# A fused encoder block on one core: order and engines of the first pair's weight splits in a Strassen-like FFN

## The chip, the cores and the metric

The kernel runs on one core of a Trainium2 chip. The metric is the device time of one execution in microseconds (us). The engines are PE (TensorE, with PEld for its weight loads), DVE (VectorE), ACT (ScalarE), POOL (GpSimd) and SP (SyncE, which here issues every DMA). Each engine works through its own list of instructions in order.

## The reference, cut to what matters

One layer: a norm, a projection into an attention part and a convolution part, their joint output projection, then the gated FFN that this change touches, and a gated embedding after it.

```python
x = x + mix @ w_out[i]
h = rmsnorm(x, ffn_norm[i])
x = x + (jax.nn.silu(h @ w_gate[i]) * (h @ w_up[i])) @ w_down[i]
gate = jax.nn.sigmoid(rmsnorm(x, ple_norm[i]) @ w_ple_gate[i])
x = x + gate * (p[i] @ w_ple_proj[i])
```

`x` is 1024 positions by 1024, all in float32; the hidden width of the FFN is 2816.

## The kernel before

**Precision.** A float32 product is made of three matmuls. `split` (L68 to L74) takes a float32 operand apart: the high part is a cast on ACT (L71), the low part a subtraction (L74) on DVE, or on POOL where the call says so. `mm3` (L78 to L80) multiplies high by high, high by low and low by high into one PSUM bank. L78 and L79 read only the high part of a weight; L80 reads its low part.

**The output projection, L673 to L709.** Eight tiles of 128 positions, t = 0 to 7. Each gets its product with `w_out` (PE), the sum with the stored half (DVE, L684), the norm (ACT L647, DVE L106, POOL L107, DVE L649). Tiles 4 to 7 are combined with tiles 0 to 3 on POOL (L702 to L705, four instructions for each), and `tsplit` transposes the results on PE (L655) and splits them into the operands B11, B21, T1, T2, T3, T4 and B22.

**The FFN's gate and up products, L731 to L823.** The hidden width is walked in 11 pairs of 128-wide blocks, p = 0 to 10. Each pair does the two products (w = 0 gate, w = 1 up) as a 2 by 2 block product with seven instead of eight block multiplications. Its weight blocks are a11, a12, a21, a22 (L737 loads them, each as two DMAs of 256 KB), its sums s1 to s4 (DVE, L752, L753, L759, L761). The products are X = a11·B11, Y = s2·T2, X += a12·B21, Z = s1·T1, Y += s3·T3, Z += s4·B22, Y += a22·T4, each for both w, 12 matmuls each. After a11·B11 the bank X is copied to `e1` by ACT (L778), before a12·B21 adds to it. Then come sums of the banks on DVE (L781, L792, L793, L796, L799), the activations, and stores. At the end of each pair, two rows of `w_down` (tiles `wd`) are loaded (L816), combined by four DVE instructions (L818 to L821) and stored (L823).

**Buffers.** Raw weight tiles have the tag `raw`, four buffers, shared by the x1 tiles of the output projection (before p = 0), the four blocks and the two `wd` tiles. Split weight tiles have the tag `whl`, eight buffers, shared by the split `w_out` blocks and by the h and l parts of a11 to s4; so four operands are held at a time. The combination tiles s1 to s4 use the tag `y`, four buffers, which hold the normed tiles 0 to 3 until these are transposed. `tm` (with `e1`) is opened after `sp3` is closed and lies over its memory; each of its tiles waits for what lies under it.

**Order.** The order of each engine's list is fixed when the kernel is built. A planner walks a simulated timeline: on each engine, of the instructions that are ready there, the one written earliest in the program goes first. So the program order is a priority, and an instruction that is ready early in the plan fills a gap. On the chip the list is run in that order, ready or not.

In the first pair (p = 0) alone, all low parts are made by POOL:

```python
            split(h, l, src, None, nc.gpsimd if p == 0 else None)
```

Of the kernel before, what the change touches and what calls it, by code (L numbers as in the profile page):

```python
# [8 lines left out]
F32 = mybir.dt.float32  # L9
F32R = mybir.dt.float32r  # L10
# [7 lines left out]
P = 128  # L18
# [33 lines left out]
def hybrid_block(ctx: ExitStack, tc: tile.TileContext, I, out):  # L52
    nc = tc.nc
    dma = nc.sync.dma_start
# [4 lines left out]
    def f32(ap):  # L59
        return ap.bitcast(F32)  # L60
# [4 lines left out]
    def sb_pool(name, side=None):  # L65
        return tc.tile_pool(name=name, bufs=1, side=side, reuse_waits="tile")

    def split(h, l, src, eng_h=None, eng_l=None):  # L68

        if eng_h is None:  # L70
            nc.scalar.copy(h, src)  # L71
        else:
            eng_h.tensor_copy(h, src)
        (eng_l or nc.vector).tensor_sub(l, src, f32(h))  # L74
# [447 lines left out]
    for h in range(NH):  # L522
# [11 lines left out]
        for c in range(2):  # L534
# [14 lines left out]
            for pr_ in range(2):  # L549
# [40 lines left out]
                if fi >= 0:  # L590
                    n = 16 - fi if h * 4 + c * 2 + pr_ == 15 else 1
# [32 lines left out]
    def tbank(name):  # L624
        bankn[0] = (bankn[0] + 1) % 4
        return bank(name, (P, 4, P), 4 + bankn[0])
# [12 lines left out]
    raws = es4.enter_context(sb_pool("raws", side="right"))  # L639
# [3 lines left out]
    sp3 = es3.enter_context(sb_pool("sp3"))  # L643
# [7 lines left out]
    def tsplit(src, hl, tt, name):  # L651

        tp = tbank(name)
        for k in range(4):
            nc.tensor.transpose(tp[:, k, :], src[:, k * P:(k + 1) * P], ident)  # L655
        ts_ = slice(tt * P, (tt + 1) * P)
        split(hl[0][:, :, ts_], hl[1][:, :, ts_], tp)
# [8 lines left out]
    def op_pair(pool, name, tag, bufs):  # L666
        return [pool.tile([P, 4, 512], F32R, name=name + w, tag=tag, bufs=bufs) for w in "hl"]


    B = {n: op_pair(mcp, n, "act", 4) for n in ("B11", "B21")}  # L670
    B |= {n: op_pair(bx, n, "bx", 6) for n in ("T2", "T1", "B22")}
    xns = []
    for t in range(NT):  # L673
        half, tt = t // 4, t % 4
        a = slice(tt * P, (tt + 1) * P)
        x1 = raws.tile([P, D], F32, name=f"x1_{t}", tag="raw", bufs=4)
        dma(x1, part_d[t * P:(t + 1) * P, :])
        for ch in range(2):
            cs = slice(ch * 512, (ch + 1) * 512)
            ps = mbank(f"po{ch}{t}")  # L680
            for k in range(NH):
                wh, wl = wsets[ch][1](k)
                mm3(ps, mA[0][half][:, k, a], mA[1][half][:, k, a], wh, wl, k == 0, k == NH - 1)
            nc.vector.tensor_add(x1[:, cs], ps, x1[:, cs])  # L684
        dma(x1_d[t], x1)
        if half == 0:
            xn = cvy.tile([P, D], F32, name=f"n2_{t}_xn", tag="y", bufs=4)
            xns.append(xn)
        else:
            xn = sp3.tile([P, D], F32, name=f"n2_{t}_xn", tag="xin", bufs=2)  # L690
        xnorm(x1, gain2, xn, sp3, f"n2_{t}")
        lo, hi = xn[:, 0:512], xn[:, 512:D]
        if half == 0:
            tsplit(lo, B["B11"], tt, f"b11_{t}")
            tsplit(hi, B["B21"], tt, f"b21_{t}")
            continue
        if tt == 0:
            B["T3"] = op_pair(map_, "T3", "act", 4)
        xa = xns[tt]
        alo, ahi = xa[:, 0:512], xa[:, 512:D]  # L700
        t2 = sp3.tile([P, 512], F32, name=f"t2_{t}", tag="t2", bufs=2)
        nc.gpsimd.tensor_sub(alo, lo, alo)  # L702
        nc.gpsimd.tensor_sub(t2, hi, alo)
        nc.gpsimd.tensor_sub(lo, hi, lo)
        nc.gpsimd.tensor_sub(ahi, ahi, t2)  # L705
        tsplit(t2, B["T2"], tt, f"tt2_{t}")
        tsplit(alo, B["T1"], tt, f"tt1_{t}")
        tsplit(lo, B["T3"], tt, f"tt3_{t}")
        tsplit(hi, B["B22"], tt, f"b22_{t}")  # L709
    B["T4"] = op_pair(map_, "T4", "act", 4)  # L710
    for tt in range(4):
        tsplit(xns[tt][:, 512:D], B["T4"], tt, f"tt4_{tt}")
# [8 lines left out]

    es5 = ExitStack()
    tm = es5.enter_context(sb_pool("tm"))
    wgs = [I[n][0].rearrange("(k p) c -> p k c", p=P) for n in ("w_gate", "w_up")]
    wds = I["w_down"][0]
    V = nc.vector

# [2 lines left out]

    for p in range(NPR):  # L731

        def blk(i, k):
            r = raws.tile([P, 2, 4, P], F32, name=f"wr{p}{i}{k}", tag="raw", bufs=4)
            f = 2 * p + i
            for w in range(2):
                dma(r[:, w], wgs[w][:, 4 * k:4 * k + 4, f * P:(f + 1) * P])  # L737
            return r

        def sop(src, name):  # L740
            h = whl.tile([P, 2, 4, P], F32R, name=f"{name}h{p}", tag="whl", bufs=8)
            l = whl.tile([P, 2, 4, P], F32R, name=f"{name}l{p}", tag="whl", bufs=8)
            split(h, l, src, None, nc.gpsimd if p == 0 else None)
            return h, l

        def comb(name):
            return cvy.tile([P, 2, 4, P], F32, name=f"{name}_{p}", tag="y", bufs=4)

        a11, a22, a21 = blk(0, 0), blk(1, 1), blk(1, 0)
        A = {"a11": sop(a11, "a11")}  # L750
        s1, s2 = comb("s1"), comb("s2")
        V.tensor_add(s1, a21, a22)  # L752
        V.tensor_sub(s2, s1, a11)  # L753
        A["s2"] = sop(s2, "s2")
        a12 = blk(0, 1)
        A["a12"] = sop(a12, "a12")
        A["s1"] = sop(s1, "s1")
        s3, s4 = comb("s3"), comb("s4")
        V.tensor_sub(s3, a11, a21)  # L759
        A["s3"] = sop(s3, "s3")  # L760
        V.tensor_sub(s4, a12, s2)  # L761
        A["s4"] = sop(s4, "s4")
        A["a22"] = sop(a22, "a22")

        def prod(ps, a, b, w, first):
            for k in range(4):
                mm3(ps, A[a][0][:, w, k, :], A[a][1][:, w, k, :], B[b][0][:, k, :], B[b][1][:, k, :],
                    first and k == 0, k == 3, not first)

        gu = range(2)  # L770
        X = [bank(f"X{p}{w}") for w in gu]
        Y = [bank(f"Y{p}{w}") for w in gu]
        e1 = [tmp(f"e1{p}{w}", f"e1{w}", 2) for w in gu]
        aa = [tmp(f"aa{p}{w}", f"aa{w}") for w in gu]
        bb = [tmp(f"bb{p}{w}", f"bb{w}") for w in gu]
        for w in gu:
            prod(X[w], "a11", "B11", w, True)
            nc.scalar.copy(e1[w], X[w])  # L778
        for w in gu:
            prod(Y[w], "s2", "T2", w, True)  # L780
            V.tensor_add(aa[w], Y[w], e1[w])  # L781
        for w in gu:
            prod(X[w], "a12", "B21", w, False)
        g11 = tmp(f"g11{p}", "g11")
        nc.scalar.activation(g11, X[0], AF.Silu)
        V.tensor_mul(g11, X[1], g11)
        Z = [bank(f"Z{p}{w}") for w in gu]
        for w in gu:
            prod(Z[w], "s1", "T1", w, True)
        for w in gu:  # L790
            prod(Y[w], "s3", "T3", w, False)
            V.tensor_add(bb[w], Y[w], e1[w])  # L792
            V.tensor_add(bb[w], Z[w], bb[w])  # L793
        for w in gu:
            prod(Z[w], "s4", "B22", w, False)
            V.tensor_add(aa[w], Z[w], aa[w])  # L796
        for w in gu:
            prod(Y[w], "a22", "T4", w, False)
            V.tensor_add(e1[w], Y[w], e1[w])  # L799

        for c in (bb, aa, e1):
            nc.scalar.activation(c[0], c[0], AF.Silu)
            V.tensor_mul(c[1], c[0], c[1])
        g22, g12, g21 = bb[1], aa[1], e1[1]

        h1, h2, h3, h4 = [tmp(f"h{i}_{p}", "hs", 4) for i in range(4)]
        V.tensor_add(h1, g12, g22)
        V.tensor_sub(h2, h1, g11)
        V.tensor_sub(h3, g11, g12)
        V.tensor_sub(h4, g21, h2)  # L810
        for i, g in enumerate((g11, g21, g22, h1, h2, h3, h4)):
            dma(ga_d[i][p], g)
        d0 = raws.tile([P, D], F32, name=f"wd{p}0", tag="raw", bufs=4)
        d1 = raws.tile([P, D], F32, name=f"wd{p}1", tag="raw", bufs=4)
        for i, d in enumerate((d0, d1)):
            dma(d, wds[(2 * p + i) * P:(2 * p + i + 1) * P, :])  # L816
        b11, b12, b21, b22 = d0[:, 0:512], d0[:, 512:D], d1[:, 0:512], d1[:, 512:D]
        V.tensor_sub(b11, b12, b11)  # L818
        V.tensor_sub(b12, b22, b12)
        V.tensor_sub(b22, b22, b11)  # L820
        V.tensor_sub(b21, b21, b22)  # L821
        for i, b in enumerate((b11, b22, b12, b21)):
            dma(wb_d[i][p], b)  # L823
# [6 lines left out]
    sp3 = es3.enter_context(sb_pool("sp3b", side="right"))  # L830
# [100 lines left out]
    A = {n: pair(n) for n in ("pa11", "pa12")}  # L931
    A["pa22"] = pair("pa22", ap)
    f11, f12, f21, fs1 = block("f11"), block("f12"), block("f21"), block("fs1")
    for t in range(NT):
# [3 lines left out]
        for k in range(2):  # L938
# [3 lines left out]
            if t < 4:  # L942
                h, l = A[("pa11", "pa12")[k]]
# [4 lines left out]
            else:  # L948
                V.tensor_add(fs1[:, :, ts_], tp, f21[:, :, ts_])
                h, l = A["pa22"]  # L950
# [139 lines left out]
```

## Time and profile before

| What | us |
|---|---|
| median of 3 runs (1289.46 to 1292.21) | 1291.48 |
| the profiled execution, its own time | 1289.18 |
| its span, first to last instruction | 1287.4 |
| PE busy | 1249.3 |
| DVE busy | 937.5 |
| POOL busy | 394.4 |

The span is the device time without 1.8 us at its ends. Times in the views are counted from the start of the span. A busy PE is not a PE at its best: matmuls overlap, and the clock that the chip grants it can be half.

### The profile page before, as it was taken

The numbers are of one execution on the slowest core, as the hardware profiler recorded it, in microseconds if no ns is written. First come the engines' busy times: TensorE is split into PE (matmuls) and PEld (weight loads), VectorE is DVE, ScalarE is ACT, GpSimd is POOL, SyncE is SP. The second block draws the span as 40 slices with busy tenths as digits, with TensorE's granted clock in tenths as the row PEclk, the third lists the DMA queues.
The fourth block names the chain that finished last, engine by engine and source line by source line (L and its number), as shares of the span: only waits on it lengthen the run. The fifth ranks groups of instructions, "written<-read, shape, count | busy, mean of one in ns | idle before, by whom it ended". The sixth has DMA issues, their size and how long they took to land.

```text
span 1287.4 us, 16537 instructions
## 1 busy us (share of the span) xinstructions
PE 1249.3 (97%) x5945; PEld 1021.1 (79%) x5945; DVE 937.5 (73%) x1220; ACT 583.0 (45%) x862; POOL 394.4 (31%) x237
## 2 busy tenths in 40 slices
PE   8999998989999999987999999999999999999998
PEld 6788877867887888866888888888888788888886
DVE  7548999868887885877667676667665576567797
ACT  7445565445776673442223232223232444346552
POOL 2459998576667661660000000000000000000230
PEclk9999999989999999988999999999999999999999
DMA  9731232496655243445444445444454997665445
GB/s 356 240 88 50 66 107 74 127 225 176 154 126 149 76 134 121 172 131 180 146 165 147 156 164 172 147 161 147 152 171 166 385 349 234 191 196 176 135 147 164
DMA packets 165079, 213.12 MB, mean 166 GB/s; under 512 B 12088, under 2 KB 90182, under 8 KB 164997
## 3 DMA queue, kind: packets, MB, share of 16 engines
q1 hardware_dynamic: 164996, 212.06, 52.0%
q8 instruction: 47, 0.77, 0.3%
q14 instruction: 36, 0.29, 0.1%
HBM read 146.41 MB, written 65.60 MB: 165 GB/s over the span
## 4 chain that ended last, share of the span: by engine, by line
PE 81%; DVE 7%; DMA 6%; issue 2%; POOL 2%; ACT 1%; SPq 1%; DVEq 0%; POOLq 0%; ACTq 0%
PE Y L78 5%; PE Y L79 5%; PE Y L80 5%; PE Z L79 3%; PE Z L78 3%; PE Z L80 3%; PE X L80 3%; PE X L78 3%; PE X L79 3%; PE dY L78 2%; PE dY L79 2%; PE dY L80 2%; PE s L562 2%; DVE acc L351 2%; PE s L563 2%
## 5 line engine op out<-in xcount | busy, mean ns | idle before, releaser
L107 POOL TENSOR_TENSOR n_r<-n_ss,mhalf 128x1 f32<-128x1 f32 x24 | 14.7, 617 | 670.1 <-DVE n_ss L106 661.6
L74 DVE TENSOR_TENSOR dl<-dr,dh 128x1024 fp32r<-128x1024 f32 x77 | 93.7, 1224 | 62.6 <-ACT dh L71 62.4
L71 ACT CAST dh<-dr 128x1024 fp32r<-128x1024 f32 x77 | 80.5, 1049 | 105.9 <-PE dY L80 37.2
L356 POOL TENSOR_TENSOR z<-z,pr 128x1024 f32<-128x1024 f32 x45 | 115.8, 2575 | 3.2 <-ACT pr L355 0.8
L351 DVE SCALAR_TENSOR_TENSOR acc<-u,cw,acc 128x1024 f32<-128x1024 f32 x71 | 91.2, 1285 | 1.5
L570 ACT ACTIVATE e<-s,nm 128x1024 f32<-128x1024 f32 x64 | 71.6, 1119 | 35.9 <-DVE nm L567 29.6
L567 DVE TENSOR_REDUCE nm<-s 128x1 f32<-128x1024 f32 x64 | 77.3, 1219 | 9.1 <-PE s L565 4.5
L579 POOL TENSOR_TENSOR e<-e,e 128x1024 f32<-128x1024 f32 x32 | 77.8, 2431 | 2.4
L355 ACT ACTIVATE pr<-u,cw 128x1024 f32<-128x1024 f32 x45 | 51.1, 1150 | 36.0 <-POOL z L356 35.6
L562 PE MATMUL s<-ka,qa 128*128 128x512 f32 x128 | 57.3, 448 | 1.6 <-ACT e L570 1.5
L578 POOL TENSOR_SCALAR e<-e,cf 128x1024 f32<-128x1024 f32 x32 | 36.9, 1153 | 65.0 <-DVE cf L577 31.9
L79 PE MATMUL dY<-dl,dh 128*128 128x512 f32 x132 | 51.5, 390 | 0.0
L563 PE MATMUL s<-kb,qb 80*128 80x512 f32 x128 | 51.4, 402 | 0.0
L80 PE MATMUL dY<-dh,dl 128*128 128x512 f32 x132 | 51.4, 389 | 0.0
L78 PE MATMUL dY<-dh 128*128 128x512 f32 x132 | 50.3, 391 | 0.0
L74 DVE TENSOR_TENSOR wtl<-wt,wth 128x512 fp32r<-128x512 f32 x64 | 43.2, 683 | 8.9 <-ACT wth L71 8.6
L71 ACT CAST wth<-wt 128x512 fp32r<-128x512 f32 x64 | 36.8, 587 | 20.6 <-PE wt L584 20.5
L796 DVE TENSOR_TENSOR aa<-Z,aa 128x512 f32<-128x512 f32 x22 | 15.2, 690 | 38.5 <-PE Z L80 38.3
L80 PE MATMUL X<-B11h,a11l 128*128 128x512 f32 x88 | 33.5, 401 | 6.5 <-DVE a11l L74 6.5
L79 PE MATMUL av<-wtl,avh 128*128 128x256 f32 x128 | 38.4, 300 | 0.0
L584 PE MATMUL wt<-ident,e 128*128 128x128 f32 x256 | 37.5, 273 | 0.3 <-DVE wtl L74 0.2
L78 PE MATMUL av<-wth,avh 128*128 128x256 f32 x128 | 37.5, 293 | 0.2 <-ACT wth L71 0.2
(396 smaller groups left out, 3984.9 us busy)
## 6 DMA issues: line engine op xcount, KB each, us to landing
dr<-ga_d SPq DMA_DIRECT2D x77, 256.0 KB, 5.6
wr<-in_w_gate SPq DMA_DIRECT2D x44, 256.0 KB, 3.0
wr<-in_w_up SPq DMA_DIRECT2D x44, 256.0 KB, 3.5
wd<-in_w_down SPq DMA_DIRECT2D x22, 512.0 KB, 3.5
wb_d<-wd SPq DMA_DIRECT2D x44, 256.0 KB, 2.0
ga_d<-h SPq DMA_DIRECT2D x44, 256.0 KB, 3.6
dr<-wb_d SPq DMA_DIRECT2D x44, 256.0 KB, 3.4
dr<-in_w_down SPq DMA_DIRECT2D x33, 256.0 KB, 3.1
```

The source lines that it names most:

```text
L71: nc.scalar.copy(h, src)
L74: (eng_l or nc.vector).tensor_sub(l, src, f32(h))
L78: nc.tensor.matmul(ps, lh, rh, start=first, stop=False, skip_group_check=more)
L79: nc.tensor.matmul(ps, lh, rl, start=False, stop=False, skip_group_check=more)
L80: nc.tensor.matmul(ps, ll, rh, start=False, stop=last, skip_group_check=more)
L351: nc.vector.scalar_tensor_tensor(acc, u[:, k:k + S], cw[:, j, k:k + 1], acc, ALU.mult, ALU.add)
L356: nc.gpsimd.tensor_add(y2, y2, pr)
L562: nc.tensor.matmul(o, qa[:, m, ts_], ka[:, m, kc * 512:(kc + 1) * 512], start=True, stop=False)
L563: nc.tensor.matmul(o, qb[:, m, ts_], kb[:, m, kc * 512:(kc + 1) * 512], start=False, stop=not diag)
L567: nc.vector.tensor_reduce(nm, sp, AX.X, ALU.max, negate=True)
L570: nc.scalar.activation(e, sp, AF.Exp, bias=nm, accum_out=s)
L579: nc.gpsimd.tensor_add(es[0], es[0], es[1])
```

## The change

In the first pair only. (1) The block a11 is loaded and split in the program right after tile t = 7's transposes, ahead of those of T4, into two tiles of its own (tag `a11`, in `sp3`) instead of two of `whl`; its low part stays on POOL. (2) The block a12 is loaded and split right after it, ahead of a22, a21 and the sums. (3) Of the low parts only that of s2 (and that of a11) stays on POOL; those of a12, s1, s3, s4 and a22 go to DVE. (4) On PE, the products a12·B21 follow directly on a11·B11, ahead of s2·T2. The other ten pairs keep their text.

```diff
+    wgs = [I[n][0].rearrange("(k p) c -> p k c", p=P) for n in ("w_gate", "w_up")]
+
+    def blk(p, i, k):
+
+        r = raws.tile([P, 2, 4, P], F32, name=f"wr{p}{i}{k}", tag="raw", bufs=4)
+        f = 2 * p + i
+        for w in range(2):
+            dma(r[:, w], wgs[w][:, 4 * k:4 * k + 4, f * P:(f + 1) * P])
+        return r
+
     xns = []
     for t in range(NT):
...
         tsplit(hi, B["B22"], tt, f"b22_{t}")
+    a11s = [sp3.tile([P, 2, 4, P], F32R, name=f"a11{w}0", tag="a11", bufs=2) for w in "hl"]
+    a11_0 = blk(0, 0, 0)
+    split(*a11s, a11_0, None, nc.gpsimd)
     B["T4"] = op_pair(map_, "T4", "act", 4)
...
         def sop(src, name):
             h = whl.tile([P, 2, 4, P], F32R, name=f"{name}h{p}", tag="whl", bufs=8)
             l = whl.tile([P, 2, 4, P], F32R, name=f"{name}l{p}", tag="whl", bufs=8)
-            split(h, l, src, None, nc.gpsimd if p == 0 else None)
+            split(h, l, src, None, nc.gpsimd if p == 0 and name == "s2" else None)
             return h, l
...
-        a11, a22, a21 = blk(0, 0), blk(1, 1), blk(1, 0)
-        A = {"a11": sop(a11, "a11")}
+        a11 = blk(p, 0, 0) if p else a11_0
+        A = {"a11": sop(a11, "a11") if p else a11s}
+        if p == 0:
+            a12 = blk(p, 0, 1)
+            A["a12"] = sop(a12, "a12")
+        a22, a21 = blk(p, 1, 1), blk(p, 1, 0)
         s1, s2 = comb("s1"), comb("s2")
         V.tensor_add(s1, a21, a22)
         V.tensor_sub(s2, s1, a11)
         A["s2"] = sop(s2, "s2")
-        a12 = blk(0, 1)
-        A["a12"] = sop(a12, "a12")
+        if p:
+            a12 = blk(p, 0, 1)
+            A["a12"] = sop(a12, "a12")
         A["s1"] = sop(s1, "s1")
...
         for w in gu:
             prod(X[w], "a11", "B11", w, True)
             nc.scalar.copy(e1[w], X[w])
+
+        for w in gu:
+            if p == 0:
+                prod(X[w], "a12", "B21", w, False)
         for w in gu:
             prod(Y[w], "s2", "T2", w, True)
             V.tensor_add(aa[w], Y[w], e1[w])
         for w in gu:
-            prod(X[w], "a12", "B21", w, False)
+            if p:
+                prod(X[w], "a12", "B21", w, False)
```

## Rows read from the trace of the kernel before

**Rows 1.** The page's shares: busy us, share of the span, instructions.
```profile
PE 1249.3 (97%) x5945; PEld 1021.1 (79%) x5945; DVE 937.5 (73%) x1220; ACT 583.0 (45%) x862; POOL 394.4 (31%) x237
```

**Rows 2.** The stages' table: each engine's busy us (x instructions), clock, DMA.
```profile
546.30:552.40 6.10, 3.95 (x29) 2.98 (x28) 5.13 (x8) 4.08 (x9) 5.00 (x4) 1.00 0.30 86
552.40:555.70 3.30, 0.63 (x4) 0.42 (x4) 3.30 (x5) 3.11 (x7) 0.00 (x0) 0.85 0.00 0
555.70:561.50 5.80, 5.76 (x13) 4.30 (x14) 5.80 (x6) 2.83 (x3) 5.73 (x2) 0.50 0.52 181
581.70:588.10 6.40, 0.00 (x0) 0.00 (x0) 3.00 (x5) 0.00 (x0) 0.00 (x0) 0.79 0.62 205
588.10:592.40 4.30, 4.23 (x10) 3.37 (x11) 1.97 (x4) 1.56 (x2) 0.00 (x0) 0.51 0.60 181
...
600.00:640.00 40.00, 40.00 (x176) 32.78 (x176) 27.29 (x35) 11.36 (x14) 0.00 (x0) 1.00 0.47 152
```

**Rows 3.** PE's waits from 540 to 605 us: total, times, longest.
```profile
PE X L80 <- DVE a11l L74: 6.5, 1, 6.5
PE Y L78 <- ACT s2h L71: 1.6, 1, 1.6
PE tt L655 <- POOL n_xn L702: 1.3, 1, 1.3
PE tt L655 <- DVE T3l L74: 1.1, 1, 1.1
PE tt L655 <- POOL t L703: 0.7, 1, 0.7
```

**Rows 4.** The chain that ended last, in order of time, from 535 us.
```profile
580.54 1.23 DVE s L759
581.78 0.37 SPq L737
582.20 3.44 DMA wr<-in_w_up
...
586.90 1.23 DVE a11l L74
588.17 0.80 PE X L80
```

**Rows 5.** POOL in order of time: the first pair's low parts (one of five left out).
```profile
535.97 2.39 POOL L74 TENSOR_TENSOR a11l<-wr,a11h 128x1024 fp32r<-128x1024 f32 x1
...
555.77 2.70 POOL L74 TENSOR_TENSOR s2l<-s,s2h 128x1024 fp32r<-128x1024 f32 x1 [4.34 <-ACT s2h L71]
558.42 3.35 POOL L74 TENSOR_TENSOR a12l<-wr,a12h 128x1024 fp32r<-128x1024 f32 x1
...
567.35 2.84 POOL L74 TENSOR_TENSOR s4l<-s,s4h 128x1024 fp32r<-128x1024 f32 x1
```

**Rows 6.** DVE in order of time, around the first two pairs.
```profile
536.03 3.40 DVE L649 SCALAR_TENSOR_TENSOR n_xn<-x,n_r,gain 128x1024 f32<-128x1024 f32 x1 [0.66 <-POOL n_r L107]
...
556.13 1.28 DVE L74 TENSOR_TENSOR T4l<-tt,T4h 128x512 fp32r<-128x512 f32 x2
557.33 2.21 DVE L761 TENSOR_TENSOR s<-wr,s 128x1024 f32<-128x1024 f32 x1
...
560.07 2.25 DVE L818 TENSOR_TENSOR wd<-wd 128x512 f32<-128x512 f32 x1
...
567.97 2.77 DVE L821 TENSOR_TENSOR wd<-wd 128x512 f32<-128x512 f32 x1
...
586.90 1.22 DVE L74 TENSOR_TENSOR a11l<-wr,a11h 128x1024 fp32r<-128x1024 f32 x1
588.09 0.69 DVE L818 TENSOR_TENSOR wd<-wd 128x512 f32<-128x512 f32 x1
```

**Rows 7.** ACT in order of time: the copies to e1, the cast of s2.
```profile
551.42 1.08 ACT L778 COPY e<-X 128x512 f32<-128x512 f32 x2
...
554.64 1.05 ACT L71 CAST s2h<-s 128x1024 fp32r<-128x1024 f32 x1
```

**Rows 8.** SP's queue: the first pair's last load, two loads of the second.
```profile
546.34 0.37 SPq L737 DMA_DIRECT2D wr<-in_w_gate  x1
...
572.88 0.37 SPq L737 DMA_DIRECT2D wr<-in_w_gate  x1
```

More of the change, by code (lines that the diff above doesn't have):

```diff
@@ L723, in hybrid_block @@
     tm = es5.enter_context(sb_pool("tm"))
-    wgs = [I[n][0].rearrange("(k p) c -> p k c", p=P) for n in ("w_gate", "w_up")]
     wds = I["w_down"][0]
@@ L731, in hybrid_block @@
     for p in range(NPR):
[L733 to L738, printed above, removed]
         def sop(src, name):
```

## The prediction

> **What bounds the kernel now.** I read the page's shares first: PE is busy 97% of the span [rows 1]. So time is won only where PE has nothing to do or runs at half its clock, and the change can only touch the stage where the FFN begins. I cut that stage into windows [rows 2]. The reader is to see four things there. From 600 to 640 us PE is never idle and does 176 matmuls in 40 us, 0.227 us each; the pairs after it look alike, so what the stage gains should reach the end. From 546.3 to 555.7 us PE is idle 6.10 − 3.95 = 2.15 and 3.30 − 0.63 = 2.67 us. From 555.7 to 561.5 us the granted clock is 0.50, the lower of the two levels, after those sparse microseconds: 13 matmuls take 5.80 us where they would take 13 × 0.227 = 2.95, so 2.85 us are lost. Then PE stands still from 581.7 to 588.1 us, and the clock is 0.51 after it: 10 matmuls in 4.30 us instead of 2.27, 2.03 us lost. With the stall at 6.5 us as the waits have it [rows 3], the stage loses 2.15 + 2.67 + 2.85 + 6.5 + 2.03 = 16.2 us. That is all there is to win here.
>
> PE's waits name the releasers [rows 3]. Early: POOL's combinations of tile 7 (1.3 and 0.7), an eviction (1.1), the cast of s2 (1.6). Late: the low part of a11 of the second pair. The chain shows why that is late [rows 4]: the sum L759 of the second pair frees a raw buffer, only then is a12 loaded, a sum that reads a12 stands in DVE's list ahead of a11's low part, and PE waits for all of it.
>
> **Why DVE is late there.** The four `wd` instructions L818 to L821 take 2.25 us (the first) and 2.77 us (each of the other three), while POOL makes low parts without a break from 555.8 to 570.2 us [rows 5, 6]. The same L818 takes 0.69 us in the second pair, with POOL idle. Each ends about half a microsecond after the POOL instruction beside it (the last: POOL to 570.19, DVE to 570.74): it waits for POOL and then runs. L761 takes 2.21 instead of 1.22 us, L649 3.40 instead of 1.28 beside POOL's a11 low part. Excess of L761 and the four: 0.99 + 1.56 + 3 × 2.08 = 8.8 us. This is on the path: L821 ends, its store lands, the second pair's block is loaded at 572.88 us [rows 8], and then the chain of [rows 4].
> The Trainium skill (SBUF — State Buffer, "Who interferes with whom") says that a VectorE instruction with two SBUF inputs and a GpSimd one that reads SBUF block each other, the second until the first is done, and that one with a PSUM input is spared. The trace agrees: the T4 low parts, from PSUM, take 1.28 us for two beside POOL's s2 [rows 5, 6].
>
> **The change part by part.**
> *Five low parts to DVE.* POOL loses five instructions of 2.4 to 3.4 us. DVE gains 5 × 1.22 = 6.1 us (the second pair's a11 low part took 1.22 [rows 6]) in a stretch where it is busy 3.30 of 3.30 and 5.80 of 5.80 us [rows 2]. It gets back up to 8.8 us. s2's low part stays on POOL, and beside it L761's 0.99 us may stay too: refund 7.8 to 8.8. How much of the 6.1 lies ahead of L821 is the planner's: all five, or only those of s1 and s3 (2.4 us), as a12's can be done before 546 us and those of s4 and a22 come late. So L821 ends 1.7 to 6.4 us earlier; I take 4.5.
>
> *a12 ahead of a22 and a21.* Four blocks, eight DMAs, as before; SP is moved past nothing but these. The four loads are released by the norms of tiles 4 to 7. a12 takes the second place (530 us), a21 the last, at 546.34 us [rows 8]. A load takes some 4 us to landing [rows 4], so a21 is there at about 550.5, and L752 (s1) could start then; it now starts at 551.5, because its buffer is freed by T4's first transposes. So 0 is lost, at most 2 us if tile 7 is late; I take 0.5. The work that would hide it is the next part.
>
> *a12·B21 ahead of s2·T2.* 24 matmuls, 24 × 0.227 = 5.5 us, which now lie behind 555.7. They add to X, so they wait for the copies to e1, which ACT makes at 551.42 to 552.5 us [rows 7], behind tile 7's casts. So they can't fill the first gap (2.15), but they fill 552.4 to 555.7 (2.67) and reach to about 558, when s2's low part is done (558.47 [rows 5]). Bounds: 0 if the copies stand behind T4's casts, 2.67 if not; I take 2.6. With PE dense from 552.5, I expect the clock not to fall: 2.85 saved, between 0 and that. Their cast on ACT (1.05) and low part on DVE move before 546 us, where ACT and DVE have gaps.
>
> *a11 early, in tiles of its own.* Before, its split stood at 534.4 to 538.4 us and its products started at 538.9, because `whl` was full of `w_out`. PE is busy until 546 either way, so its products gain nothing. But POOL's instruction held L649 of tile 6 for 2.12 us, on the path to tile 7's transposes. Earlier, it lies in another gap and holds tile 5 instead, whose transposes wait for PE. Gain 0 to 2.1; I take 1.0, off the first gap. It frees two `whl` buffers: s4 takes a12's, and the second pair's a11 takes s1's, as now.
>
> *Second stall.* PE reaches it 1.0 + 2.6 + 2.85 − 0.5 = 5.9 us earlier, so the 4.5 us of DVE alone would leave it longer, not shorter. What decides is the order in DVE's list. In the plan, a11's low part of the second pair is ready when s1·T1 is done, and the bank sums L792 and L793 of the first pair when s3·T3 is. Both move about 5.5 us earlier, with the 24 matmuls, against the second pair's a12, whose loads wait for a DVE list that is up to 6.1 us longer in the plan (if the plan knows nothing of the blocking, it had no refund to lose). So they should now stand ahead of L761 of the second pair, and PE goes on with s4·B22 and a22·T4 (48 matmuls, 10.9 us), by which time the second pair's s2 is split. Then 6.5 and 2.03 us are saved. Bounds: all of it, or nothing. I take all, less 2.0 us for remaining short waits.
> The Trainium skill (TensorE: Matmul & The Clock Gate, the specification table) has VectorE's queue as strictly first in, first out. That rule speaks against moving five instructions there; the wait of 6.5 us behind L761 agrees with it.
>
> *Sum.* 1.0 + 2.6 + 2.85 − 0.5 + 6.5 + 2.03 − 2.0 = 12.5 us. The profiled execution took 1289.18 us, so 1276.7. The runs' median lies 2.3 us above it; against that, 1291.5 − 12.5 = 1279.0.
>
> **The rivals.**
> (A, the forecast) Both stalls go: 10 to 16.2 us, up to 18 with all of POOL's 2.1: 1273.5 to 1281.5. Chance 0.52.
> (B) One stall stays. If a11's low part or L792 stays behind L761 in DVE's list, PE still waits for the second pair's a12. The gain is then what L821's end moves, 1.7 to 6.4 us, whatever the first gap gives: 1285 to 1290, 1287 in the middle. For it: it is the order now, and SP's and DVE's in-order lists carry any delay on. Against it: the shift of some 11 us between the two in the plan. If instead the copies to e1 are late and the first gap stays, the second stall's 8.5 less 2.0 remains: 1285. Chance 0.30.
> (C) The cover is lost elsewhere: a new wait of 10 us or more eats it, such as a raw buffer that comes free one step later (one step was 572.88 to 581.78, 8.9 us [rows 4, 8]). About 1289 to 1294. Chance 0.08.
> (D) Slower: DVE is the bound. All 6.1 us lie ahead of L821 and the refund doesn't come, because what held L818 to L821 was not POOL. Then the second pair's a12 and with it the end come up to 6.1 us later: 1297.6. It turns to a loss from a refund below 6.1 us, and to one of over 0.2% (2.6 us, about what a measurement of this kernel can tell from no change) from one below 3.5 us. For it: DVE has no free microsecond from 552 to 561. Against it: 0.69 against 2.77 us for the same instruction, and its ends that follow POOL's. Chance 0.10.
>
> **How the numbers follow.** The time is A's, 1279.0. A and B hold 0.82, so the range runs from 1273.5 to 1289; A's own is 1273.5 to 1281.5. Faster by over 0.2% is below 1288.9: A, nearly all of B, a little of C: 0.81. Within 0.2%: 0.09. Slower: 0.10.
>
> **What the profile of the changed kernel would show.** L818 to L821 of the first pair at 0.7 us each, and L649 of tile 6 near 1.3. X's L80 with a12 ahead of Y's, and no half clock near 556 us. Idle PE from 546 to 556 us below 2.5 us. a11's low part of the second pair ahead of L761 in DVE's order, and no PE wait over 2 us from 575 to 595. I am wrong if DVE's low part stands behind a sum that waits for a load (B), or if the four `wd` instructions stay long (D).

## The result, and the profile after

The changed kernel takes 1276.2 us (median of four runs, 1275.05 to 1280.21); the kernel before, run beside it, 1290.47 (1289.35 to 1292.21). The ratio is 0.9898, 95% interval 0.9882 to 0.9914: 13.2 us of 1290.47. The profiled execution took 1275.05 us against 1289.18, 14.1 less. The forecast was 12.5 us less, 1279.0.

The page's shares after [rows 1]:

```profile
PE 1245.3 (98%) x5945; PEld 1020.0 (80%) x5945; DVE 931.8 (73%) x1225; ACT 582.7 (46%) x862; POOL 377.3 (30%) x232
```

PE has the same 5945 instructions. POOL has five fewer and DVE five more, and yet DVE is busy 5.7 us less, because the instructions that were held beside POOL no longer are.

The gain lies in one stage. Its length is taken here from the last transposes ahead of the output projection (PE L516) to the first matmul of the down product (dX). PE in order of time, before:

```profile
507.58 0.60 PE L516 MATMUL hb<-ident,on 128*128 128x128 f32 x4
...
984.84 0.86 PE L78 MATMUL dX<-dh 128*128 128x512 f32 x3
```

That is 477.3 us. After:

```profile
507.24 0.60 PE L516 MATMUL hb<-ident,on 128*128 128x128 f32 x4
...
971.13 0.86 PE L78 MATMUL dX<-dh 128*128 128x512 f32 x3
```

That is 463.9 us, 13.4 less. What lies ahead of 507 us is the work of other stages and differs by up to 5 us between executions of any of these kernels; so each experiment below has its stage's length beside its time. Each length is that of one profiled execution; two whose engines run the same lists, the changed kernel and e3 below, agree to 0.04 us.

The stages' table after, with the same columns and edges as [rows 2], and one window more:

```profile
546.30:552.40 6.10, 3.43 (x27) 2.93 (x28) 5.35 (x9) 3.24 (x8) 5.01 (x4) 1.00 0.30 86
552.40:555.70 3.30, 2.96 (x15) 2.26 (x14) 3.30 (x5) 2.31 (x6) 0.00 (x0) 1.00 0.00 0
555.70:561.50 5.80, 5.80 (x29) 4.81 (x28) 4.17 (x5) 5.05 (x6) 2.41 (x1) 1.00 0.52 181
...
580.00:590.00 10.00, 10.00 (x45) 8.19 (x44) 8.60 (x13) 2.58 (x4) 0.00 (x0) 1.00 0.69 238
```

PE's waits from 540 to 605 us, as [rows 3]:

```profile
PE tt L655 <- POOL n_xn L712: 2.0, 1, 2.0
PE tt L655 <- POOL n_xn L714: 0.6, 1, 0.6
PE X L78 <- ACT e L788: 0.3, 1, 0.3
PE tt L655 <- POOL t L713: 0.2, 1, 0.2
```

Read against the windows of before: from 546.3 to 552.4 us PE is idle 2.67 instead of 2.15 us, 0.5 worse (a further 0.18 us of this gap lies just ahead of 546.3). From 552.4 to 555.7 it is idle 0.34 instead of 2.67, 2.3 better. The granted clock stays at 1.00, the upper level, through 561.5; the 2.85 us of the half clock are gone. From 555.7 to 600 us PE is never idle (the row of 580 to 590 stands for those between); the stall of 6.5 and the 2.03 us at half clock behind it are gone. The sum is −0.5 + 2.3 + 2.85 + 6.5 + 2.03 = 13.2 us, and the stage is 13.4 shorter. Nothing is given back later.

DVE in order of time (the lines of `wd` are L833 to L836 now, the sums L761 to L771, the bank sums L807 and L808):

```profile
...
569.26 0.68 DVE L836 TENSOR_TENSOR wd<-wd 128x512 f32<-128x512 f32 x1
571.08 1.22 DVE L74 TENSOR_TENSOR a11l<-wr,a11h 128x1024 fp32r<-128x1024 f32 x1 [1.14 <-ACT a11h L71]
572.97 0.69 DVE L807 TENSOR_TENSOR bb<-Y,e 128x512 f32<-128x512 f32 x1 [0.67 <-PE Y L80]
575.52 1.23 DVE L761 TENSOR_TENSOR s<-wr,wr 128x1024 f32<-128x1024 f32 x1 [1.86 <-DMA wr<-in_w_up]
...
580.13 1.21 DVE L771 TENSOR_TENSOR s<-wr,s 128x1024 f32<-128x1024 f32 x1
```

The reader is to see two things: the `wd` instructions take 0.69 us, not 2.25 to 2.77 [rows 6], and the second pair's a11l stands ahead of its sums, 9 us ahead of the sum L771 that reads a12. Before, that sum (L761 there) stood right ahead of a11l, at 585.75 us.

### The profile page after: what moved, and what is told of

Its sections match the earlier page's. It is cut to its first block, busy times and chain, and to the rows that moved or that the text cites. A ratio compares the mean times of both kernels' runs of the same rounds, so it can differ in the third digit from the quotient of the medians.

```text
span 1273.3 us, 16528 instructions
## 1 busy us (share of the span) xinstructions
PE 1245.3 (98%) x5945; PEld 1020.0 (80%) x5945; DVE 931.8 (73%) x1225; ACT 582.7 (46%) x862; POOL 377.3 (30%) x232
## 4 chain that ended last, share of the span: by engine, by line
PE 83%; DVE 6%; DMA 4%; POOL 3%; issue 2%; ACT 1%; SPq 0%; DVEq 0%; POOLq 0%; ACTq 0%
PE Y L78 5%; PE Y L79 5%; PE Y L80 5%; PE Z L79 3%; PE Z L78 3%; PE Z L80 3%; PE X L78 3%; PE X L79 3%; PE X L80 3%; PE dY L78 2%; PE dY L79 2%; PE dY L80 2%; PE s L562 2%; DVE acc L351 2%; PE s L563 2%
## 5 line engine op out<-in xcount | busy, mean ns | idle before, releaser
L80 PE MATMUL av<-wth,avl 128*128 128x256 f32 x128 | 36.3, 284 | 0.0
```

Of the source, the lines that this page charges most:

```text
L80: nc.tensor.matmul(ps, ll, rh, start=False, stop=last, skip_group_check=more)
```

## The experiments

Times are medians with the ratio to the kernel before, run on the same chip. None of them leaves out or changes part of the computation; one adds work that nothing uses.

| Kernel | us | ratio (95%) | stage, us | stage against before |
|---|---|---|---|---|
| changed kernel | 1276.2 | 0.9898 (0.9882 to 0.9914) | 463.9 | −13.4 |
| e1: before, low parts on DVE | 1282.85 | 0.9934 (0.9914 to 0.9955) | 469.1 | −8.1 |
| e2: changed, low parts on POOL | 1289.05 | 0.9978 (0.9965 to 0.9991) | 475.4 | −1.9 |
| e3: changed, a12's products written late | 1277.1 | 0.9886 (0.9858 to 0.9914) | 463.9 | −13.3 |
| e4: changed, a11 split in its old place | 1277.8 | 0.9893 (0.9871 to 0.9914) | 464.5 | −12.7 |
| e5: before, s4 behind the bank sums | 1292.27 | 1.0006 (0.9993 to 1.002) | 477.9 | +0.6 |
| e6: changed, two of tile 7's combinations on DVE | 1280.85 | 0.9912 (0.9885 to 0.994) | 465.6 | −11.6 |
| e7: changed, a11's low part on DVE | 1278.16 | 0.9903 (0.989 to 0.9915) | 464.9 | −12.4 |
| e9: changed, unused POOL work added | 1284.47 | 0.9946 (0.9931 to 0.996) | 470.3 | −7.0 |
| e11: changed, e1 in tiles of its own | 1280.21 | 0.9918 (0.9905 to 0.9931) | 466.9 | −10.3 |
| e13: e11, with a11's and s2's low parts on DVE | 1279.97 | 0.992 (0.9908 to 0.9932) | 467.7 | −9.5 |

**e1: part 3 alone.** The kernel before, with the engines of the low parts as in the changed one.

```diff
-            split(h, l, src, None, nc.gpsimd if p == 0 else None)
+            split(h, l, src, None, nc.gpsimd if p == 0 and name in ("a11", "s2") else None)
```

> The kernel before with only the five low parts moved to DVE (a12 stays third, its products after s2's). My theory, two separate losses: the second stall and the half clock behind it (6.5 + 2.0 us) go, because L818 to L821 take 0.7 us each and a11's low part of the second pair stands ahead of L761; the first gap and its half clock (2.15 + 2.67 + 2.85 us) stay. 8 us less than before, about 1282 us, a saving of 7 to 9 us. Rival, the order comes only from the 24 matmuls moved ahead: the stall at 582 us stays over 4 us and the saving is below 4 us. Rival, DVE is the bound: slower than before by up to 6 us.

1282.85 us, 8.5 less by the ratio. PE's waits from 540 to 605 us have no second stall:

```profile
PE Y L78 <- ACT s2h L71: 1.6, 1, 1.6
PE tt L655 <- POOL n_xn L702: 1.4, 1, 1.4
...
```

(The lines left out are the first gap's too, 1.1 and 0.7.) The first gap and the half clock behind it (0.55 from 555.7 to 561.5 us) stay. DVE in order of time shows why the stall went:

```profile
567.41 0.68 DVE L821 TENSOR_TENSOR wd<-wd 128x512 f32<-128x512 f32 x1
...
577.53 1.22 DVE L74 TENSOR_TENSOR a22l<-wr,a22h 128x1024 fp32r<-128x1024 f32 x1
...
580.94 1.22 DVE L74 TENSOR_TENSOR a11l<-wr,a11h 128x1024 fp32r<-128x1024 f32 x1
582.84 1.22 DVE L761 TENSOR_TENSOR s<-wr,s 128x1024 f32<-128x1024 f32 x1 [0.69 <-DMA wr<-in_w_up]
```

a11's low part stands ahead of L761 here too. The second stall and its half clock are 6.5 + 2.03 = 8.5 us; the stage is 8.1 shorter. The ratio's interval runs from 5.8 to 11.1 us, so its 8.5 is not good to a tenth. The rival that DVE would be the bound falls: it took five more instructions of 1.22 us, and its last `wd` of the first pair ended at 568.09, 2.65 us earlier than before, though the stage began 1.3 us later in this execution.

**e2: all parts but part 3.**

```diff
-            split(h, l, src, None, nc.gpsimd if p == 0 and name == "s2" else None)
+            split(h, l, src, None, nc.gpsimd if p == 0 else None)
```

> The changed kernel with the five low parts back on POOL (a11 early, a12 second, its products first). My theory: the first gap is filled and the clock stays up there, as in the changed kernel (5 us saved), but the four wd instructions take over 2 us each beside POOL and the second pair's blocks come late, so PE waits again for a11's low part or the bank sums, 5 us or more, between 574 and 590 us. About 1285 us, 4 to 8 us less than before. Rival, the second stall is gone by the 24 matmuls' move alone: about 1277 us, as the changed kernel.

1289.05 us: 2.8 less than before, short of what was expected. PE's waits, one row of the stages' table, and DVE in order of time:

```profile
PE X L80 <- DVE a11l L74: 5.4, 1, 5.4
PE tt L655 <- POOL n_xn L712: 2.9, 1, 2.9
PE Y L78 <- DVE aa L795: 1.9, 1, 1.9
```

```profile
552.40:555.70 3.30, 3.20 (x20) 2.80 (x20) 2.51 (x4) 2.22 (x4) 2.27 (x2) 0.65 0.07 21
```

```profile
571.86 2.77 DVE L836 TENSOR_TENSOR wd<-wd 128x512 f32<-128x512 f32 x1
...
582.64 1.23 DVE L761 TENSOR_TENSOR s<-wr,wr 128x1024 f32<-128x1024 f32 x1 [6.82 <-DMA wr<-in_w_up]
...
586.25 1.22 DVE L74 TENSOR_TENSOR a11l<-wr,a11h 128x1024 fp32r<-128x1024 f32 x1
587.39 1.22 DVE L771 TENSOR_TENSOR s<-wr,s 128x1024 f32<-128x1024 f32 x1
```

PE is busy 3.20 of 3.30 us from 552.4 to 555.7, where the second gap was, but against the expectation the granted clock did not stay up: it is 0.91 from 546.3 to 552.4 and 0.65 in this window, and 1.00 again from 555.7 us until the late stall. And the `wd` instructions take 2.28 to 2.77 us again, the second pair's blocks land late, and PE waits 5.4 + 1.9 us for DVE. The rival that the shift of the 24 matmuls alone cures the stall falls; a11's low part even stands ahead of L771, the sum that reads a12, and PE waits all the same. Alone, parts 1, 2 and 4 are worth 2.8 us and part 3 is worth 8.5, together 13.2; the medians can't tell that from the sum of 11.3, but the stages, 1.9 and 8.1 against 13.4, say that it is more. What the first parts give comes through only when DVE is not late.

**e9: the blocking put back.** Four unused subtractions on POOL, where four of the low parts were.

```diff
+    scr = tm.tile([P, 2, 4, P], BF16, name="scr")
...
             split(h, l, src, None, nc.gpsimd if p == 0 and name == "s2" else None)
+            if p == 0 and name in ("s1", "s3", "s4", "a22"):
+                nc.gpsimd.tensor_sub(scr, src, f32(h))
```

> The changed kernel with four POOL subtractions added beside it in the first pair: they read the same operands of s1, s3, s4 and a22 as DVE's low parts do and write a scratch tile that nobody uses; DVE's list is unchanged and the result too. My theory, POOL blocks DVE: DVE's instructions with two SBUF inputs between 560 and 575 us (low parts, wd) take 2 us and more where a POOL one runs beside them, the last wd instruction ends 4 to 8 us later, and a good part of the second stall comes back: 1279 to 1285 us. Rival, the long wd instructions of the kernel before had another cause (loads, the place in the list): they stay at 0.7 us and the time at 1276 within 1.5 us.

1284.47 us. Nobody reads `scr`, and DVE's list of work is the same. POOL's added instructions and DVE, each in order of time:

```profile
564.12 3.44 POOL L752 TENSOR_TENSOR scr<-s,s1h 128x1024 bf16<-128x1024 f32 x1 [0.45 <-ACT s1h L71]
...
570.98 3.26 POOL L752 TENSOR_TENSOR scr<-s,s4h 128x1024 bf16<-128x1024 f32 x1
```

```profile
565.21 3.42 DVE L775 TENSOR_TENSOR s<-wr,s 128x1024 f32<-128x1024 f32 x1
568.56 0.68 DVE L805 TENSOR_TENSOR g<-X,g 128x512 f32<-128x512 f32 x1
...
571.91 2.88 DVE L837 TENSOR_TENSOR wd<-wd 128x512 f32<-128x512 f32 x1
```

One DVE instruction with two inputs from SBUF (the engines' main memory) gets through per POOL instruction: L837 ends at 574.79, 0.55 us after POOL's at 574.24. L805, which reads the bank X, takes its 0.68 us while POOL runs. PE then waits 4.6 us for DVE's `aa`. From 564 to 583 us DVE waits for no other engine and no load, so late loads or buffers did not make it late. So the work beside, not a longer list of DVE's, is what costs: 6.4 us of stage (470.3 against 463.9). The Trainium skill (SBUF — State Buffer, "Who interferes with whom") says that the one which issues first holds the shared ports for its whole instruction; these rows agree for DVE's two-SBUF-input instructions.

**e5: the order of DVE's list alone.** The kernel before, with s4 of the second pair issued behind the first pair's bank sums.

```diff
-        V.tensor_sub(s4, a12, s2)
+        with tc.issue_after(bb_last.ins) if p == 1 else nullcontext():
+            V.tensor_sub(s4, a12, s2)
...
-            V.tensor_add(bb[w], Z[w], bb[w])
+            bb_last = V.tensor_add(bb[w], Z[w], bb[w])
```

> The kernel before, with one ordering alone added: the second pair's sum s4 (L761 of before) goes behind the first pair's second bank sum in DVE's list. Nothing else moves, POOL keeps all low parts. My theory: the second stall is the in-order wait behind that sum, so a11's low part follows on the third sum at about 582 us, and PE waits 1 to 2 us in place of 6.5; the half clock behind it goes too or is shorter. 5 to 7 us less than before, about 1285 us. Rival, the wait is DVE's lateness itself (wd beside POOL) and not the order: a saving below 2 us.

1292.27 us, no gain: this theory fell. PE's waits and DVE in order of time (lines are one higher than before's, L819 is the first `wd`):

```profile
PE Y L78 <- DVE bb L793: 4.7, 1, 4.7
PE X L80 <- DVE a11l L74: 2.2, 1, 2.2
```

```profile
585.23 1.21 DVE L74 TENSOR_TENSOR a11l<-wr,a11h 128x1024 fp32r<-128x1024 f32 x1
591.89 0.69 DVE L819 TENSOR_TENSOR wd<-wd 128x512 f32<-128x512 f32 x1 [5.45 <-DMA wd<-in_w_down]
592.50 0.68 DVE L793 TENSOR_TENSOR bb<-Y,e 128x512 f32<-128x512 f32 x1
```

a11's low part came ahead, as wanted, and PE's wait for it fell from 6.5 to 2.2 us. But then a `wd` of the second pair, which waits for its own load, stood ahead of the bank sums, and PE waited 4.7 us there: 6.9 us in all. With DVE and the loads late, the wait moved to another instruction of DVE's list that waits for a load.

**e3 and e4: parts 4 and 1 undone.** e3 leaves a12's products behind s2's in the program; e4 splits a11 in its old place, into `whl`.

```diff
# e3
-            if p == 0:
-                prod(X[w], "a12", "B21", w, False)
...
-            if p:
-                prod(X[w], "a12", "B21", w, False)
+            prod(X[w], "a12", "B21", w, False)
# e4
-    a11s = [sp3.tile([P, 2, 4, P], F32R, name=f"a11{w}0", tag="a11", bufs=2) for w in "hl"]
-    a11_0 = blk(0, 0, 0)
-    split(*a11s, a11_0, None, nc.gpsimd)
...
-            split(h, l, src, None, nc.gpsimd if p == 0 and name == "s2" else None)
+            split(h, l, src, None, nc.gpsimd if p == 0 and name in ("a11", "s2") else None)
...
-        a11 = blk(p, 0, 0) if p else a11_0
-        A = {"a11": sop(a11, "a11") if p else a11s}
+        a11 = blk(p, 0, 0)
+        A = {"a11": sop(a11, "a11")}
```

> The changed kernel with a12's products of the first pair left at their old place in the program, behind Y's first ones (part 4 undone). Theory: the planner puts them ahead of s2's products by itself, since a12 is split early, so every engine's list is that of the changed kernel and the time is the same, 1276 to 1278 us. Rival: the text's order matters for the time: the 2.3 us of the second gap and the 2.85 us of the half clock come back, about 1281 us.

> The changed kernel with a11's split in its old place and in whl's tiles, low part still on POOL. My theory after the result: the early split gains nothing, since the first gap is not shorter with it; the time is that of the changed kernel within 1.5 us, with the gap of PE between 546 and 552 us at 2 to 3 us. Rival, the early split is part of the gain (tiles of its own free two whl buffers, or L649 of tile 6 is freed): 2 us or more above the changed kernel.

e3: 1277.1 us and the same 463.9 us of stage; each engine's list of instructions is the changed kernel's. The planner had put the products first by itself, since a12 is split early. e4: 1277.8 us, a ratio of 0.9893 against 0.9898: no difference. Its first gap is one wait of 2.4 us for tile 7, shorter than the changed kernel's, but with the granted clock at 0.78 and 0.89 in the first two windows instead of 1.00. So parts 1 and 4, each undone by itself, are worth nothing that can be measured. That leaves the early split of a12 (part 2) beside the low parts on DVE (part 3, e1); part 2 was not undone by itself.

**e7: a11's low part off POOL.**

```diff
-    split(*a11s, a11_0, None, nc.gpsimd)
+    split(*a11s, a11_0)
```

> The changed kernel with a11's low part on DVE too. Theory: what is left of the first gap (3.2 us of waits in the changed kernel) waits for POOL's combinations of tiles 5 to 7, which a11's 3.4 us on POOL push back; on DVE they run earlier and the gap shrinks by 1 to 2.5 us: 1274 to 1275.5 us. Rival, tile 7 is late for another reason (PE, its norm): no difference, 1276.

1278.16 us, no gain. The waits of the first gap shrink from 2.0 + 0.6 + 0.2 to 1.5 + 0.4 + 0.4 us, and a new one of 1.0 us for a11's low part stands at 619 us, in the third pair: the lists have changed there too.

**e11 and e13: the first gap filled.** The copies to `e1` are what keeps a12's products out of the first gap: `tm` lies over `sp3`. e11 gives the first pair's `e1` tiles in a pool of their own; e13 moves a11's and s2's low parts to DVE besides.

```diff
+    es7 = ExitStack()
+    ee = es7.enter_context(sb_pool("ee"))
     sp3 = es3.enter_context(sb_pool("sp3"))
...
-        e1 = [tmp(f"e1{p}{w}", f"e1{w}", 2) for w in gu]
+        e1 = [(ee, tm)[p % 2].tile([P, 512], F32, name=f"e1{p}{w}", tag=f"e1{w}", bufs=1) for w in gu]
# e13 also
-    split(*a11s, a11_0, None, nc.gpsimd)
+    split(*a11s, a11_0)
...
-            split(h, l, src, None, nc.gpsimd if p == 0 and name == "s2" else None)
+            split(h, l, src, None, None)
```

> The changed kernel with the e1 tiles of even pairs in a small pool of their own that lies over nothing (still two per w in all). Theory: a12's products wait for the copies to e1, and these for the memory of tile 7's tiles; with their own memory the copies stand at about 545 us, a12's products fill the first gap, PE's waits between 545 and 553 us fall from 3.2 us to below 1.5: 1274 to 1275 us. Rival, the gap moves on: what is no longer idle before 553 us is idle after it, waiting for s2, and the time stays at 1276.

> The changed kernel with the e1 tiles as in the version before, and the low parts of a11 and s2 on DVE as well, so that POOL makes none. Theory: both gains add as far as the gap lasts, 3 us at most: 1273 us. Rival: s2's low part on DVE stands behind other work in DVE's list, and PE waits for it: 1275 to 1277 us.

Both are slower than the changed kernel, 1280.21 and 1279.97 us; the intervals of the ratios overlap a little, but the stages are 3.0 and 3.8 us longer. The stages' table of e11 and its PE waits:

```profile
546.30:552.40 6.10, 6.10 (x36) 5.27 (x35) 3.68 (x5) 2.64 (x5) 4.62 (x6) 1.00 0.27 81
552.40:555.70 3.30, 3.21 (x23) 2.71 (x22) 0.90 (x2) 1.52 (x4) 2.22 (x2) 1.00 0.04 10
555.70:561.50 5.80, 2.29 (x16) 1.52 (x15) 5.80 (x9) 4.48 (x9) 0.00 (x0) 1.00 0.12 45
```

```profile
PE Y L78 <- ACT s2h L71: 3.3, 1, 3.3
PE tt L657 <- DVE T3l L74: 1.2, 1, 1.2
```

The first gap is full, PE 6.10 of 6.10 us. But PE now does the products ahead of tile 7's transposes, T4 and s2 come later (s2's high part is done 53.1 us into the stage, in the changed kernel 49.3), and PE waits 3.3 us for it, with the granted clock at 0.80 from 561.5 to 570 us. The gap moved on. The same 24 matmuls are worth more at the end of the gap, over the wait for s2. In e13 PE waits 2.8 us for s2's high part and 0.2 for its low part; neither its theory (1273 us) nor its rival (1275 to 1277) came about.

**e6: tile 7's chain shortened.**

```diff
-        nc.gpsimd.tensor_sub(alo, lo, alo)
-        nc.gpsimd.tensor_sub(t2, hi, alo)
+        (nc.vector if tt == 3 else nc.gpsimd).tensor_sub(alo, lo, alo)
+        (nc.vector if tt == 3 else nc.gpsimd).tensor_sub(t2, hi, alo)
```

> The changed kernel with the first two of tile 7's four combinations on the vector engine instead of POOL. Theory: what is left of the first gap (2.67 us idle of 546.3 to 552.4) is the chain of tile 7: its norm, two POOL combinations in a row, then the transposes; on DVE each takes about half the time, so PE waits 1 to 2 us less there and the time is 1274.5 to 1275.5 us. Rival: the gap moves on to the next late operand, s2's high part, as it did where the copies to e1 had tiles of their own: 1276 us or more, no difference that can be told.

No gain; its runs spread from 1276.5 to 1285.7 us, and the stage is 465.6 us. DVE in order of time:

```profile
550.18 1.28 DVE L649 SCALAR_TENSOR_TENSOR n_xn<-x,n_r,gain 128x1024 f32<-128x1024 f32 x1 [3.38 <-POOL n_r L107]
...
551.98 0.68 DVE L74 TENSOR_TENSOR T2l<-tt,T2h 128x512 fp32r<-128x512 f32 x1
552.58 0.68 DVE L712 TENSOR_TENSOR n_xn<-n_xn,n_xn 128x512 f32<-128x512 f32 x1
```

The combination takes 0.68 us on DVE where POOL's takes 1.27, but it stands behind two low parts of tile 6. It ends 1.8 us after the norm (551.46 to 553.26), and PE goes on at 553.40, 1.9 us after it; in the changed kernel PE goes on 1.4 us after the norm (546.74 to 548.14). PE's wait is 2.6 us instead of 2.0. So the first gap is not shorter, and it did not move to s2's high part, as the rival had it. PE does wait 0.5 us for s2's low part, which took POOL 3.37 us beside DVE's L771.

## Why the prediction was right

The time lies in the range, and case A came about: both stalls went. That the sum of 12.5 was within 0.7 us of the 13.2 is partly luck: 2.0 us too little for the second stall against 1.0 too much for the first gap and 0.3 for the second. Term by term:

**Second stall: 6.5 + 2.03, as forecast.** e1 shows it by itself: 8.1 us of stage, 8.5 by the ratio. The 2.0 us kept back for remaining short waits were not needed: PE has none from 553 to 600 us. Right in kind: `wd` takes 0.69 us, and a11l and the first pair's sums L807 stand ahead of the sum that reads a12.

**What brought a11l in time: the reason given was only half of it.** The prediction let the order in DVE's list decide, and the 24 matmuls' move bring that order. The order does not decide by itself: e2 has a11l ahead of the sum that reads a12 and PE waits 5.4 us, and e5 forces that order and gains nothing. Nor does it need the move: e1 has it without. What the stall's end needs is that DVE and the loads behind it are not late (e1, e9). The worry that PE comes too early for DVE's gain alone was right, though. In e1, a11l ends 73.3 us into the stage and PE uses it at 74.1; in the changed kernel PE uses it at 69.3, so in e1's place it would be some 4 us late (an estimate from these rows; not tried). In the changed kernel a11l ends at 65.1, ahead of all of its pair's sums. Neither e1 nor e2 has it so far ahead; it came there only with the move and the low parts on DVE together.

**"L821 ends 4.5 us earlier": mis-sized.** It ends at 569.94 instead of 570.74 us, 0.8 earlier, below the bounds of 1.7 to 6.4. The planner put all four remaining low parts (s1, s3, s4, a22) ahead of it, 4 × 1.22 = 4.9 us, and `g` and `aa` besides (0.69 + 1.28), which stood behind L821 before. And DVE waited 1.6 us for the cast of s1, where before it had no wait from 552 us to L821. DVE in order of time, before:

```profile
570.67 1.27 DVE L781 TENSOR_TENSOR aa<-Y,e 128x512 f32<-128x512 f32 x2
...
581.67 0.69 DVE L786 TENSOR_TENSOR g<-X,g 128x512 f32<-128x512 f32 x1
```

and after:

```profile
559.38 1.23 DVE L74 TENSOR_TENSOR s1l<-s,s1h 128x1024 fp32r<-128x1024 f32 x1 [1.63 <-ACT s1h L71]
```

The forecast had its own bound for all of the low parts; the other work that was free to move in, and the wait for ACT, had no price.

**What this left out: the load of the second pair's a12.** The prediction let it wait for the sum that frees a buffer, as in [rows 4]. In the changed kernel it doesn't. SP in order of time, around that load:

```profile
570.29 0.46 SPq L838 DMA_DIRECT2D wb_d<-wd  x1
570.79 0.43 SPq L679 DMA_DIRECT2D wr<-in_w_up  x1
574.78 0.37 SPq L679 DMA_DIRECT2D wr<-in_w_gate  x1
```

The waits of SP's queue put 3.5 us ahead of it down to a store of the first pair's `wd`. It is issued at 574.78 instead of 581.78 us [rows 4], 7.0 us earlier, though L836 ends only 0.8 us earlier. In e1 it is issued at 578.78, right after the low part of the first pair's a22 (577.53 + 1.22), and in e2 at 577.77, 3.1 us after L836's end. So what a12's load waits for differs from kernel to kernel, also between the kernel before and e1, whose blocks have the same order. That is read from what its load waited for; what decides how the buffers are dealt out was not tried. The stall's end doesn't hang on this load: in e1 and in the changed kernel a11l is made before a12 has landed.

**Fill of the second gap: 2.6 forecast, 2.3 measured**, with the first product at 553.04 us, behind the copies to `e1`, as the prediction had it. The half clock's 2.85 us were saved in full; with the gap left open, in e1, the clock fell again to 0.55.

**a11 early: +1.0 forecast; it saved nothing.** The first gap grew by 0.5 us, tile 7 and the last load together, for which 1.0 − 0.5 had been taken. POOL in order of time:

```profile
528.30 3.38 POOL L74 TENSOR_TENSOR a11l<-wr,a11h 128x1024 fp32r<-128x1024 f32 x1
...
535.51 2.28 POOL L715 TENSOR_TENSOR n_xn<-n_xn,t 128x512 f32<-128x512 f32 x1
```

Tile 6's L649 took 1.28 us instead of 3.40, as forecast. But a11's low part took 3.38 us beside tile 5's L649 (DVE, 1.55), and L715 took 2.28 instead of 1.3 beside a12's low part on DVE. Each holds POOL's combinations, and through them the next tile's norm. The excess was moved from DVE to POOL on the same chain. e4 and e7 show that its place and its engine matter little: 463.9 to 464.9 us of stage in all three.

**What would have shown it right** all came, but one: idle PE from 546 to 556 us is 3.2 us, not below 2.5, by the first gap.

**The rivals.** B (one stall stays) is what e2 and e5 look like: 2.8 us saved, and none. D (DVE is the bound) fell with e1. B's ground, that in-order lists carry any delay on, is what e2 and e5 show; what decided for A is that DVE was no longer late.

## What to carry to other kernels

When two engines each have free time on average, look at which of their instructions run side by side: a helper that holds the other can cost more than the work it takes over. A stall behind one instruction of an in-order list can be the sign that the whole list is late; moving that instruction (e5) then moves the stall to another. Work that fills a gap does not belong ahead of the work whose results the gap is waiting for (e11).

## What the runs showed of the hardware

The holding goes both ways. A POOL subtraction of 128 by 1024 took 2.41 us with no two-input DVE work from SBUF beside it (s2's, at 556.58 us in the changed kernel), 3.38 beside DVE's L649, 3.37 in e6 beside L771 and 3.44 in e9; a combination of 128 by 512 took 2.28 us instead of 1.3. In the prediction, that POOL is the one that is made to wait had no price. DVE in order of time, beside that combination:

```profile
535.17 1.47 DVE L74 TENSOR_TENSOR a12l<-wr,a12h 128x1024 fp32r<-128x1024 f32 x1
```

It starts 0.34 us ahead of the combination (535.51) and is itself 0.25 us longer than its usual 1.22.
